# A hybrid attention block on one core: stores moved some steps behind their tiles, the loads of one value pass spread evenly, and eight chains shifted by five steps

## The chip, the cores and the metric

The kernel runs on one core of one Trainium2 chip. A core has a matrix engine (PE, with its weight loads listed as PEld), a vector engine (DVE), an activation engine (ACT), a general engine (POOL) and a sync engine (SP), and 16 DMA engines that move data between its working memory and the chip's main memory. SP, ACT and POOL each issue DMAs from their own queue of instructions. The metric is the time of one execution in microseconds (us), as the median of several runs; a profile of one more execution is beside it. Times inside an execution are counted from the start of its span.

## The reference

512 tokens of width 2048 go through one layer. `h = rmsnorm(x)` is projected by one wide matrix into the operands of two mixers and two gates; the mixers' outputs are projected, gated, merged, projected again and added to the residual.

```python
h = rmsnorm(x, norm_gain)
proj = h @ w_in
(aq, ak, av, az, iq, ik, iw, rq, rk, rv, rz, ga, gb) = jnp.split(proj, SPLIT_POINTS, axis=-1)
a_out = dsa_mixer(aq, ak, av, iq, ik, iw, positions, rel_bias) * jax.nn.silu(az)
b_out = retention_mixer(rq, rk, rv, ret_gn_gain) * jax.nn.silu(rz)
merged = jax.nn.sigmoid(ga) * (a_out @ w_a_out) + jax.nn.sigmoid(gb) * (b_out @ w_b_out)
r = x + merged @ w_o
return r + (p_i @ w_ple) * jax.nn.sigmoid(r @ w_ple_gate)      # then a last rmsnorm
```

Mixer A selects 128 keys for each query by an index score (`lax.top_k`) and attends to them with a bias that depends on the distance; mixer B is a retention with 8 heads in chunks of 64 tokens. All is float32. The kernel gets that precision from matmuls of a reduced form: each operand is split into a high part and a low part, and three products are added.

## The kernel before, in words

**Stages, in order of time.** (1) The index projection and its scores. (2) Four *values passes* (`values`, L685): two for the retention's values `rv`, two for the attention's values `av`. In a pass the split activations `hparts` (16 pairs of tiles, one pair per block k of the width) are the stationary operands, and a weight unit of 2 k is the moving one; k runs over 16 blocks, and for each k four token tiles t get three matmuls each. So a pass has 16 x 4 = 64 steps in 8 weight units, and ends with four accumulators that `normal` (L703, on ACT) scales out of PSUM. (3) 24 *pairs* (`gemm_pair`, L213): for each of 8 retention heads, one pair for its queries and keys, and two for gates. A pair computes two 128-column blocks of the projection with seven products of half size instead of eight; the products `s3, a11, a12, s4, s2, a22, s1` each have their own moving operands `Xh`, 8 tiles each, 56 in all. A product is one weight unit: 8 matmuls with the high weights and 8 with the low ones, 8 steps; a pair has 56 steps. (4) More pairs for `rz`, attention's `q`, `k` and `az`, then the attention heads and the output projections.

**The moving parts.** The 56 tiles of `Xh` are made from `x` in the background of the first passes (`combos`, L266) and stored to main memory (`hd`). `x_load(count)` (L824, issued by SP) brings them back, in the order of the products. Before, the third pass (i = 0) asks for `s // 4` tiles after block s, that is none in blocks 0 to 3 and three per block in 12 to 15, 24 in all; the fourth pass (i = 1) asks for two per block, 32. They take slots of one pool of 69 tiles (`U`, L51), which also holds `hparts`, the values' results and most scratch tiles. A slot is taken again only when the last user of its tile is done, a store among them; so the loads of the fourth pass also take slots that `hparts` leave.

**The order of work is written by hand.** The program's order on each engine is the order in which the Python code issues, and each engine takes its instructions in that order. `step()` (L164) is called after each group of matmuls; `later(n, f)` issues f n steps later. A background list `bg` (L154) holds the rest: the 48 steps that make the moving parts, 48 rounds of the top-k selection (L597 to L604, DVE), the mask's copy and store (`mask_store`, L609), and 160 steps that build the position bias (masks on DVE, L616; 12 small matmuls on PE, L630; a copy and a store on ACT, L633 to L637). One entry is issued every `state["rate"]` steps: 2 in the values passes, 20 in the 24 pairs, 9 after.

**Weights.** `load_to` (L106) has SP load blocks of 512 KB into 7 buffers, some units ahead of use; `split_to` (L121) has ACT write the high part `wh` (L136) two units ahead of its matmuls and one step later DVE the low part `wl` (L141); each has 3 buffers. In a pair, three of the seven units add another block of weights to the buffer: `add_block` (L102) does it with an accumulating DMA on POOL's queue.

**Around the change.** At the end of each `av` pass ACT scales the first accumulator to `avh`, stores it, then stores `avl`, which DVE makes from the same accumulator (L840), and so on for three token tiles; the fourth is stored whole (L837). The next pass, or the first pair, is issued after these. `retention(h)` (L713) hands its steps to `later` when the head's second output is there: `queries` (DVE), `scores` (PE, `ps_rs` L744), `keys`, `decay`, `states`, `values_out`, `norm` (with a POOL instruction, L796), `scale` and `back`, after which SP stores `yd` (L813). Before, `scores` comes 19 steps and `norm` 52 steps after it; the rotation of queries and keys ends on DVE with the instruction of L730, 7 steps after it. `b_load` (L1014) brings mixer B's result back for its output projection and 25 steps later has it split.

Of the kernel before, what the change touches and what calls it, by code (L numbers as in the profile page):

```python
# [9 lines left out]
F32 = mybir.dt.float32  # L10
F32R = mybir.dt.float32r
# [3 lines left out]
OP = mybir.AluOpType  # L15
# [5 lines left out]
NT = L // 128  # L21
# [13 lines left out]
def block_kernel(tc, xT, pT, posb, posq, w_in, w_v, w_ik, w_a, w_b, w_o, w_ple, w_gate,  # L35
                 w_gt, w_pt, fgb, tab, gains, cst, dec, out, out_a, out_b):
    nc = tc.nc
    pe, dve, act, pool, sp = nc.tensor, nc.vector, nc.scalar, nc.gpsimd, nc.sync

    with contextlib.ExitStack() as ctx:  # L40
# [10 lines left out]
        def U(name, dt=F32):  # L51
            return up.tile([128, L], dt, name=name, tag="u")
# [19 lines left out]
        state = {"raw": 0, "split": 0, "rate": BG_RATE}  # L72
# [85 lines left out]
        def later(n, f):  # L158
            if n <= 0:
                return f()  # L160
            tick[1] += 1
            heapq.heappush(soon, (tick[0] + n, tick[1], f))
# [153 lines left out]
        u_rv, u_av = ([block(w_v[i], (2,) * 8, 512) for i in g] for g in ((0, 1), (2, 3)))  # L316
# [24 lines left out]
        for k in range(KT):  # L341
            if k in (1, 2, 4, 8, 12):
                load_to(state["raw"] + 1)
            if k < 10:
                t = U("xk")
                sp.dma_start(t, xT[:, k, :])
                xs.append(t)
            elif k % 2 == 0:
                t = B("xk2")
# [92 lines left out]
        R = {}  # L442
# [164 lines left out]
        mnd = dp.tile([128, 1280], F32, name="mnd")  # L607

        def mask_store():  # L609
            t = B("mf")  # L610
            dve.tensor_copy(t, mneg)
            later(2, lambda: sp.dma_start(mnd, t))

        bias_e = {}

# [69 lines left out]
        def values(ids, name, each=lambda s: None):  # L685

            pss = [P("ps_vn") for _ in range(NT)]
            seq = ksteps(ids)
            for s, (i, k) in enumerate(seq):
                if k == 0:  # L690
                    split_to(i + AHEAD)
                    load_to(i + AHEAD + LOADS)
                h, l = loaded[i]
                a, b = hparts[s]
                for t in range(NT):
                    pe.matmul(pss[t], a[:, tok(t)], h[:, k], start=(s == 0), stop=False)  # L696
                    pe.matmul(pss[t], a[:, tok(t)], l[:, k], start=False, stop=False)  # L697
                    pe.matmul(pss[t], b[:, tok(t)], h[:, k], start=False, stop=(s == KT - 1))  # L698
                    step()
                each(s)  # L700
            return pss

        def normal(ps, name, t, dt=F32):  # L703
            v = U(name, dt)
            act.activation(v, ps, AF.Copy, scale=R["nat"][:, t:t + 1])
            return v
# [3 lines left out]
        vd = dp.tile([2, 7, 128, L], F32, name="vd")  # L710
        rd = dp.tile([2, NT, 128, L], F32, name="rd")

        def retention(h):  # L713
# [44 lines left out]
            def keys(i):  # L758
                if i == 0:
                    E["pk"] = turn(E[1], 3)  # L760
                else:
                    E["kn"] = U("kn")
                    act.activation(E["kn"][:, 0:384], E["pk"], AF.Copy, scale=dect[:, 256:257])

            def states(i):
                if i == 0:
                    ps = E["ps"] = P("ps_kv")
                    for t in range(3):
                        pe.matmul(ps[:, tok(t)], E["kn"][:, tok(t)], rv[:, tok(t)], start=True, stop=True)
                elif i == 1:  # L770
                    E["s"] = U("state")
                    act.activation(E["s"][:, 0:128], E["ps"][:, 0:128], AF.Copy)
                else:
                    for t in (1, 2):
                        dve.scalar_tensor_tensor(E["s"][:, tok(t)], E["s"][:, tok(t - 1)], g128, E["ps"][:, tok(t)],
                                                 op0=OP.mult, op1=OP.add)

            def values_out(t):
                if t == 0:
                    E["py"] = P("ps_y")  # L780
                    E["st"] = S("gst", 24)
                    E["mv"] = S("gmv", 8)
                o = E["py"][:, tok(t)]
                pe.matmul(o, E["at"][:, tok(t)], rv[:, tok(t)], start=True, stop=(t == 0))
                if t:
                    pe.matmul(o, E["qt"][:, tok(t - 1)], E["s"][:, tok(t - 1)], start=False, stop=True)
# [20 lines left out]
            def back(i):  # L807
                if i == 0:
                    E["pt"] = turn(E["yn"], NT)
                else:  # L810
                    E["yT"] = U("yT")
                    act.activation(E["yT"], E["pt"], AF.Copy, scale=gn[:, h:h + 1])
                    later(2, lambda: sp.dma_start(yd[h], E["yT"]))  # L813

            steps = [(9, queries), (19, scores), (21, lambda: keys(0)), (22, decay), (24, lambda: keys(1))]
            steps += [(n, lambda i=i: states(i)) for i, n in enumerate((34, 36, 38))]
            steps += [(46 + t, lambda t=t: values_out(t)) for t in range(NT)]
            steps += [(52, norm), (62, scale), (74, lambda: back(0)), (77, lambda: back(1))]
            return rotate

        Xh = {n: [None] * 8 for n in PRODUCTS}
# [2 lines left out]
        def x_load(count):  # L824
            while x_wanted and count:
                n, k = x_wanted.popleft()
                Xh[n][k] = U("h" + n, F32R)
                sp.dma_start(Xh[n][k].bitcast(F32), x_at[n, k])
                count -= 1
# [2 lines left out]
            for t, ps in enumerate(values(u_rv[i], "rv")):  # L832
                act.dma_start(rd[i, t], normal(ps, "rv", t))
        for i in range(2):
            for t, ps in enumerate(values(u_av[i], "av", lambda s, i=i: x_load(2 * i or s // 4))):
                if t == NT - 1:
                    act.dma_start(vd[i, 6], normal(ps, "av", t))  # L837
                    continue
                vh, vl = normal(ps, "avh", t, F32R), U("avl", F32R)
                dve.scalar_tensor_tensor(vl, ps, R["nat"][:, t:t + 1], vh.bitcast(F32), op0=OP.mult, op1=OP.subtract)  # L840
                act.dma_start(vd[i, 2 * t], vh.bitcast(F32))
                act.dma_start(vd[i, 2 * t + 1], vl.bitcast(F32))
        for i in range(len(x_wanted)):
            later(1 + 2 * i, lambda: x_load(1))
        state["rate"] = BG_RATES[1]


# [51 lines left out]
        av = []  # L899
# [114 lines left out]
        def b_load(h):  # L1014
            t = U("bk")
            sp.dma_start(t, bd[h])
            later(25, lambda: bparts.append(split(t, "b", 1)))

        for n in range(NH // 2):
            if n == NH // 2 - 1:  # L1020
                while bg:
                    bg.popleft()()
                for h in range(NH):
                    later(10 + 3 * h, lambda h=h: b_load(h))
                heads = [attention_head(h) for h in range(NH)]
                later(38, heads[0].pop(0)[1])
            gate_pair(u_az[n], to(zd[2 * n:2 * n + 2], AF.Silu))
# [27 lines left out]
        for m in PAIRED:  # L1055
            t = B("sm")
            s, o = t[:, 0:512], t[:, 512:1024]
# [17 lines left out]
        for m in range(8):  # L1075
# [13 lines left out]
            if m == 7:  # L1089
                todo.extend([None] * 24)  # L1090
                for k in range(2):
                    t = U("pk")
# [9 lines left out]
        for m in range(MF):  # L1102
            i = u_p[m // 4][0]
# [3 lines left out]
            h, l = loaded[i]  # L1107
            ps = P("ps_pw")
# [270 lines left out]
```

## Time and profile before

| what | value |
|---|---|
| median of 3 runs | 1722.48 us (1719.68 to 1722.67) |
| profiled execution, its own time | 1720.52 us |
| its span, first to last instruction | 1718.7 us |
| mean granted clock of PE | 0.994 |
| DVE, ACT, POOL busy | 1265.3, 867.3, 219.6 us |
| moved by DMA | 361.76 MB, 210 GB/s over the span |

The page gives each engine's busy time, the chain of work that ended last, and the costliest groups of instructions. A group's line gives the source line, engine, operation, output and inputs, the count, the busy time, and after the bar the idle time before it with what ended it. Other views are used too: the waits (who waited for whom, in all, how often, the longest), the timeline (start, length, instruction, and in square brackets the idle time before it and what ended it; "ACTq" and "SPq" are DMA issues from those queues), and windows (busy time of each engine, PE's granted clock as a share of full speed, and the mean busy share of the 16 DMA engines, in a stretch of time). Matmuls are pipelined: the start of one to the start of the next is what it takes, not its listed length.

### The profile page before, as it was taken

How to read it: one execution, taken by the hardware profiler on the slowest of the kernel's cores; microseconds unless marked ns; L12 is line 12 of the kernel's file. 1: busy time of each engine (PE TensorE's matmuls, PEld its weight loads, DVE VectorE, ACT ScalarE, POOL GpSimd, SP SyncE). 2: the span in 40 equal slices, each digit the busy share in tenths (PEclk: the TensorE clock that was granted, in tenths of full speed). 3: DMA queues.
4: the chain of work that ended last, by engine and by line, in shares of the span. 5: the costliest groups of instructions: out<-in, count | busy, mean ns of one | idle time of the engine just before them, and what ended most of it. 6: DMA issues, size and time to landing. Idle time of an engine off the chain costs nothing.

```text
span 1718.7 us, 25053 instructions
## 1 busy us (share of the span) xinstructions
PE 1690.7 (98%) x9334; PEld 1454.1 (85%) x9334; DVE 1265.3 (74%) x2007; ACT 867.3 (50%) x1288; POOL 219.6 (13%) x224
## 2 busy tenths in 40 slices
PE   9999989999999999999999999999999999999997
PEld 7988877788888888888888888888888888888896
DVE  7787985777878778877787776776668877864453
ACT  7465422455555555555555545566644444463342
POOL 2100000111111111111331111100000111112222
PEclk9999999999999999999999999999999999999999
DMA  7338979787787787787898888899856688732222
GB/s 283 123 116 293 355 269 293 201 219 198 190 220 201 193 215 201 194 214 206 229 236 232 224 214 222 229 309 366 273 201 205 172 214 223 205 121 100 91 68 98
DMA packets 136665, 361.76 MB, mean 210 GB/s; under 512 B 14944, under 2 KB 27232, under 8 KB 136544
## 3 DMA queue, kind: packets, MB, share of 16 engines
q1 hardware_dynamic: 98176, 251.63, 42.1%
q0 software_dynamic: 22528, 82.85, 26.8%
q10 hardware_dynamic: 15840, 25.70, 4.2%
q8 instruction: 73, 1.20, 0.3%
q14 instruction: 48, 0.39, 0.1%
HBM read 306.51 MB, written 53.61 MB: 210 GB/s over the span
## 4 chain that ended last, share of the span: by engine, by line
PE 81%; DVE 8%; DMA 7%; ACT 2%; issue 1%; SPq 0%; ACTq 0%; POOL 0%; DVEq 0%; POOLq 0%
PE ps_p L258 22%; PE ps_v L258 14%; PE ps_r L258 8%; PE ps_q L258 7%; PE ps_pg L198 3%; PE ps_pg L197 3%; PE ps_pg L196 3%; PE ps_w L197 2%; PE ps_w L196 2%; PE ps_w L198 2%; DVE isc L601 1%; DVE wl L141 1%; PE ps_iq L196 1%; PE ps_iq L197 1%; PE ps_iq L198 1%
## 5 line engine op out<-in xcount | busy, mean ns | idle before, releaser
L141 DVE TENSOR_TENSOR wl<-wraw,wh 128x1024 fp32r<-128x1024 f32 (+2 forms) x459 | 560.3, 1229 | 234.2 <-ACT wh L136 227.6
L136 ACT ACTIVATE wh<-wraw 128x1024 fp32r<-128x1024 f32 (+2 forms) x459 | 474.3, 1042 | 250.7 <-DVE wraw L143 116.1
L104 POOL DMA_DIRECT2D wraw<-w_in x120 | 105.8, 943 | 914.3 <-DVE wl L141 352.1
L224 ACT ACTIVATE e<-ps_p 128x512 f32<-128x512 f32 x144 | 86.1, 598 | 176.8 <-PE ps_p L258 174.4
L258 PE MATMUL ps_p<-hs,wh 128*128 128x512 f32 x640 | 161.5, 393 | 0.0
L258 PEld LDWEIGHTS ps_p<-hs,wh 128*128 128x128 f32 x640 | 114.7, 189 | 21.6 <-issue 1.3
L696 PE MATMUL ps_vn<-wh,hh 128*128 128x512 f32 x256 | 101.3, 396 | 4.7 <-ACT wh L136 4.7
L697 PE MATMUL ps_vn<-wl,hh 128*128 128x512 f32 x256 | 100.9, 394 | 0.5 <-DVE wl L141 0.5
L698 PE MATMUL ps_vn<-wh,hl 128*128 128x512 f32 x256 | 100.6, 393 | 0.0
L258 PE MATMUL ps_p<-hs,wl 128*128 128x256 f32 x640 | 96.6, 287 | 0.0
L258 PE MATMUL ps_q<-ha,wh 128*128 128x512 f32 x320 | 84.5, 401 | 3.4 <-ACT wh L136 3.4
L258 PEld LDWEIGHTS ps_p<-hs,wl 128*128 128x128 f32 x640 | 83.9, 192 | 1.1 <-issue 1.1
L258 PE MATMUL ps_p<-ha,wh 128*128 128x512 f32 x320 | 80.8, 393 | 0.0
L258 PE MATMUL ps_r<-hs,wh 128*128 128x512 f32 x320 | 80.5, 393 | 0.0
L258 PE MATMUL ps_v<-ha,wh 128*128 128x512 f32 x320 | 80.3, 391 | 0.0
L258 PE MATMUL ps_v<-hs,wh 128*128 128x512 f32 x320 | 79.6, 390 | 0.0
L198 PE MATMUL ps_pg<-rh,wl 128*128 128x512 f32 x192 | 74.8, 390 | 0.0
L197 PE MATMUL ps_pg<-rl,wh 128*128 128x512 f32 x192 | 74.7, 389 | 0.0
L196 PE MATMUL ps_pg<-rh,wh 128*128 128x512 f32 x192 | 74.7, 389 | 0.0
L857 DVE TENSOR_TENSOR go<-e_t 128x256 f32<-128x256 f32 x160 | 68.0, 425 | 5.6
L258 PEld LDWEIGHTS ps_v<-ha,wh 128*128 128x128 f32 x320 | 59.8, 188 | 13.6 <-issue 1.2
L258 PEld LDWEIGHTS ps_v<-hs,wh 128*128 128x128 f32 x320 | 59.9, 188 | 13.1 <-ACT wh L136 0.4
(352 smaller groups left out, 3521.5 us busy)
## 6 DMA issues: line engine op xcount, KB each, us to landing
wraw<-w_in SPq DMA_DIRECT2D x174, 512.0 KB, 4.9
wraw<-w_in POOLq DMA_DIRECT2D x120, 512.0 KB, 7.6
wraw<-w_v SPq DMA_DIRECT2D x32, 512.0 KB, 4.5
wraw<-w_o SPq DMA_DIRECT2D x32, 512.0 KB, 4.9
wraw<-w_o POOLq DMA_DIRECT2D x24, 512.0 KB, 6.8
wraw<-w_gate SPq DMA_DIRECT2D x24, 512.0 KB, 3.8
hd<-hs SPq DMA_DIRECT2D x32, 256.0 KB, 4.7
hs<-hd SPq DMA_DIRECT2D x32, 256.0 KB, 5.5
```

The source lines that it names most:

```text
L104: pool.dma_start(out=raw_tiles[r], in_=src[:, k0:k0 + 8, :], accum_op=OP.add)
L136: act.activation(h, raw, AF.Copy)
L141: dve.tensor_sub(l, raw, h.bitcast(F32))
L196: pe.matmul(o, h[:, k, w], a, start=(s == order[0]), stop=False)
L197: pe.matmul(o, h[:, k, w], b, start=False, stop=False)
L198: pe.matmul(o, l[:, k, w], a, start=False, stop=(s == order[-1]))
L224: act.activation(E[n], src, AF.Copy)
L258: pe.matmul(o[:, c], w[:, k], X[PRODUCTS[n]][k][:, c], start=(n < 4 and part == 0 and k == 0), stop=(part == parts[1] and k == 7), skip_gr ...
L696: pe.matmul(pss[t], a[:, tok(t)], h[:, k], start=(s == 0), stop=False)
L697: pe.matmul(pss[t], a[:, tok(t)], l[:, k], start=False, stop=False)
L698: pe.matmul(pss[t], b[:, tok(t)], h[:, k], start=False, stop=(s == KT - 1))
L857: dve.tensor_add(o[:, q], c0, c1)
```

## The change

It edits six places.

- `mask_store`: the DMA that stores the mask is issued 20 steps after the copy that makes its tile, not 2.
- `retention`: `scores` and all later steps of a head come 5 steps later (19 to 24, and so on to 77 to 82); `queries` stays at 9.
- The third pass asks for one moving part per block k (16 in all, before 24), the fourth for two as before (32); the 8 that remain, all of the last product `s1`, are asked for in the first pair, one every 3 steps.
- In the fourth pass the background goes at one entry per 4 steps (`BG_RATE`), not 2.
- After an `av` pass, the four `normal` instructions are issued on ACT one behind the other, then the three `avl` on DVE, and the seven stores are issued on ACT 8, 10, ... 20 steps later.
- `b_load`: head h at 4 + 3h steps, before 10 + 3h.

```diff
         def mask_store():
             t = B("mf")
             dve.tensor_copy(t, mneg)
-            later(2, lambda: sp.dma_start(mnd, t))
+            later(20, lambda: sp.dma_start(mnd, t))
...
-            steps = [(9, queries), (19, scores), (21, lambda: keys(0)), (22, decay), (24, lambda: keys(1))]
-            steps += [(n, lambda i=i: states(i)) for i, n in enumerate((34, 36, 38))]
-            steps += [(46 + t, lambda t=t: values_out(t)) for t in range(NT)]
-            steps += [(52, norm), (62, scale), (74, lambda: back(0)), (77, lambda: back(1))]
+            steps = [(9, queries), (24, scores), (26, lambda: keys(0)), (27, decay), (29, lambda: keys(1))]
+            steps += [(n, lambda i=i: states(i)) for i, n in enumerate((39, 41, 43))]
+            steps += [(51 + t, lambda t=t: values_out(t)) for t in range(NT)]
+            steps += [(57, norm), (67, scale), (79, lambda: back(0)), (82, lambda: back(1))]
...
         for i in range(2):
-            for t, ps in enumerate(values(u_av[i], "av", lambda s, i=i: x_load(2 * i or s // 4))):
-                if t == NT - 1:
-                    act.dma_start(vd[i, 6], normal(ps, "av", t))
-                    continue
-                vh, vl = normal(ps, "avh", t, F32R), U("avl", F32R)
-                dve.scalar_tensor_tensor(vl, ps, R["nat"][:, t:t + 1], vh.bitcast(F32), op0=OP.mult, op1=OP.subtract)
-                act.dma_start(vd[i, 2 * t], vh.bitcast(F32))
-                act.dma_start(vd[i, 2 * t + 1], vl.bitcast(F32))
+            if i:
+                state["rate"] = BG_RATE
+            pss = values(u_av[i], "av", lambda s, i=i: x_load(i + 1))
+            vs = [normal(ps, "av", t, F32 if t == NT - 1 else F32R) for t, ps in enumerate(pss)]
+            for t in range(NT - 1):
+                vl = U("avl", F32R)
+                dve.scalar_tensor_tensor(vl, pss[t], R["nat"][:, t:t + 1], vs[2 * t].bitcast(F32), op0=OP.mult,
+                                         op1=OP.subtract)
+                vs.insert(2 * t + 1, vl)
+            for j, v in enumerate(vs):
+                later(8 + 2 * j, lambda v=v, j=j, i=i: act.dma_start(vd[i, j], v if j == 6 else v.bitcast(F32)))
         for i in range(len(x_wanted)):
-            later(1 + 2 * i, lambda: x_load(1))
+            later(1 + 3 * i, lambda: x_load(1))
...
                 for h in range(NH):
-                    later(10 + 3 * h, lambda h=h: b_load(h))
+                    later(4 + 3 * h, lambda h=h: b_load(h))
```

## The prediction

> **What bounds the kernel now.** I read the page first, for the engine that is full, and the chain of work that ended last.
>
> ```profile
> PE 1690.7 (98%) x9334; PEld 1454.1 (85%) x9334; DVE 1265.3 (74%) x2007; ACT 867.3 (50%) x1288; POOL 219.6 (13%) x224
> PE 81%; DVE 8%; DMA 7%; ACT 2%; issue 1%; SPq 0%; ACTq 0%; POOL 0%; DVEq 0%; POOLq 0%
> q1 hardware_dynamic: 98176, 251.63, 42.1%
> q0 software_dynamic: 22528, 82.85, 26.8%
> ```
>
> PE is full, and the change takes no matmul away. So it can only give back time in which PE stands or runs slowly, and the second view is PE's own waits.
>
> ```profile
> PE ps_vn L696 <- ACT wh L136: 4.7, 1, 4.7
> PE ps_rs L744 <- DVE go L730: 4.1, 3, 3.5
> PE ps_q L258 <- ACT wh L136: 3.4, 1, 3.4
> PE ps_w L197 <- DVE bl L676: 1.5, 1, 1.5
> PE ps_bias L630 <- DVE mk L622: 0.6, 1, 0.6
> ```
>
> Five short rows, 14.3 us together, and each is at a place that the diff touches. But a wait costs more than its length, which PE's timeline shows around the first of them, in the fourth values pass:
>
> ```profile
> 247.44 0.39 PE L698 MATMUL ps_vn<-wh,hl 128*128 128x512 f32 x1
> 252.55 0.80 PE L696 MATMUL ps_vn<-wh,hh 128*128 128x512 f32 x1 [4.72 <-ACT wh L136]
> ...
> 254.40 0.63 PE L698 MATMUL ps_vn<-wh,hl 128*128 128x512 f32 x1
> 254.83 0.63 PE L696 MATMUL ps_vn<-wh,hh 128*128 128x512 f32 x1
> ...
> 258.65 0.40 PE L696 MATMUL ps_vn<-wh,hh 128*128 128x512 f32 x1
> ```
>
> After the stop the starts are 0.43 us apart until 258.65, where a clean pass has 0.227 (43.5 us for its 192 matmuls). From 247.44 to 258.65 there are 13 intervals, which should take 2.9 us and take 11.2: the wait of 4.7 costs 8.3. The next view gives whole pairs: the first rows below are the starts of the first, second, and third pair of head 0, then the second and third pair of head 1, then the last pair before the output projection and that projection.
>
> ```profile
> 290.96 0.63 PE L258 MATMUL ps_v<-hs,wh 128*128 128x512 f32 x2
> 315.66 0.98 PE L258 MATMUL ps_v<-hs,wh 128*128 128x512 f32 x3
> 326.82 2.04 PE L744 MATMUL ps_rs<-go 128*128 128x128 f32 x8 [3.45 <-DVE go L730]
> 344.53 0.62 PE L258 MATMUL ps_v<-hs,wh 128*128 128x512 f32 x2
> ...
> 384.50 0.62 PE L258 MATMUL ps_v<-hs,wh 128*128 128x512 f32 x2
> 408.27 0.62 PE L258 MATMUL ps_v<-hs,wh 128*128 128x512 f32 x2
> ...
> 1117.75 0.62 PE L258 MATMUL ps_v<-hs,wh 128*128 128x512 f32 x2
> 1137.27 0.39 PE L196 MATMUL ps_w<-bh,wh 128*128 128x512 f32 x1
> ```
>
> A clean pair takes 1137.27 - 1117.75 = 19.5 us; the first takes 24.7, so 5.2 too much. Head 1's second pair, which carries a head's retention steps, takes 23.8; head 0's takes 28.9, 5.1 too much. In pairs a step is 19.5 / 56 = 0.35 us, in values passes 43.5 / 64 = 0.68 us.
>
> **The change part by part.** *Stores behind their tiles, third pass.* Why ACT was late with `wh` stands in ACT's and DVE's timelines:
>
> ```profile
> 235.67 0.33 ACTq L841 DMA_DIRECT2D vd<-avh  x1
> 246.22 0.33 ACTq L842 DMA_DIRECT2D vd<-avl  x1
> 246.60 0.69 ACT L705 ACTIVATE avh<-ps_vn,r_nat 128x512 fp32r<-128x512 f32 x1 [10.96 <-DVE avl L840]
> ...
> 251.44 2.95 ACT L136 ACTIVATE wh<-wraw 128x1024 fp32r<-128x1024 f32 x3 [0.40 <-ACT av L705]
> ```
>
> ```profile
> 239.43 1.22 DVE L141 TENSOR_TENSOR wl<-wraw,wh 128x1024 fp32r<-128x1024 f32 x1
> 245.44 0.75 DVE L840 SCALAR_TENSOR_TENSOR avl<-ps_vn,r_nat,avh 128x512 fp32r<-128x512 f32 x1
> ```
>
> DVE runs about 10 us behind (the selection rounds at one entry per 2 steps fill it), the store of `avl` stands on ACT until DVE is there, and three `wh` stand behind it. After the change four `normal` at 0.69 us end near 238, and `wh` of the pass's unit 2 follows at once; PE wants it at 247.7. The same seven stores are still issued, but 5.4 to 13.6 us later, when their tiles exist; behind each stands `wh` of a unit that PE wants 10 us later. What is late next is DVE: three `avl` at 0.75 from 245.44, then `wl` of unit 2 at 1.22, done at 248.9, and PE wants it 0.23 after 247.7. That leaves a wait of 1.0 us, with 0 (if DVE is a little less behind) and 3.5 (if a little more) as ends. With one entry per 4 steps DVE then has 1.2 + 2 x 1.1 us of work per unit of 5.4 and catches up. **Gain 8.3 - 1.0 = 7.3.** The slower rate moves three bias groups out of this pass; they and their matmuls are issued later, so that is worth only the wait of 0.6 on `mk`: **0.6**.
>
> *First and second pair.* The windows show what the DMA engines did:
>
> ```profile
> 237.00:247.00 10.00, 10.00 (x46) 8.27 (x45) 8.95 (x21) 0.40 (x1) 0.00 (x0) 1.00 0.40 137
> ...
> 291.00:316.00 25.00, 21.59 (x114) 18.33 (x113) 11.25 (x14) 10.19 (x14) 0.89 (x1) 0.93 1.00 326
> ```
>
> The last two columns are the share of the DMA engines and GB/s. They are at 0.40 in the stretch in which ACT's store is held, and at 1.00 from 291 to 316, when what was not asked for earlier comes at once. What holds SP's queue besides is in its waits:
>
> ```profile
> SPq L813 <- ACT yT L812: 127.6, 8, 16.9
> SPq L612 <- DVE mk L622: 11.5, 1, 11.5
> ```
>
> ```profile
> 272.60 0.32 SPq L612 DMA_DIRECT2D mnd<-mf  x1
> ```
>
> The mask's store keeps SP waiting for 11.5 us up to 272.6, and the loads behind it bunch up. In the first pair the weights then land late, and ACT and DVE are late for the rotation:
>
> ```profile
> 306.15 0.89 POOL L104 DMA_DIRECT2D wraw<-w_in  x1 [17.46 <-DMA wraw<-w_in]
> ```
>
> ```profile
> 314.55 2.01 ACT L136 ACTIVATE wh<-wraw 128x1024 fp32r<-128x1024 f32 x2 [3.82 <-DMA wraw<-w_in]
> ```
>
> With the store 20 steps behind its copy, the loads spread, and the stores off the end of the pass, the causes of the 5.2 and the 5.1 go. In their place come, all in the first pair, the eight `s1` tiles (steps 1 to 22), the seven `vd` stores (steps 8 to 20) and the mask's store: of the 32 background entries of the fourth pass before, 12 were selection rounds and the next was the mask's copy; at one per 4 steps the copy comes at step 52 of 64, and its store at step 8 of the pair. Their price follows from the queues. On q1 a MB takes 0.421 x 1718.7 / 251.63 = 2.88 us of all 16 engines, on q0, which carries POOL's adding loads, 0.268 x 1718.7 / 82.85 = 5.6.
>
> ```profile
> wraw<-w_in POOLq DMA_DIRECT2D x120, 512.0 KB, 7.6
> hs<-hd SPq DMA_DIRECT2D x32, 256.0 KB, 5.5
> vd<-avh ACTq DMA_DIRECT2D x6, 256.0 KB, 4.8
> ```
>
> Up to the last `s1` tile: 8 tiles and 7 stores of 0.26 MB, the mask 0.66, the head's constants and values 0.4, three weight blocks 1.6 make 6.6 MB or 19 us, one adding load 2.9: 22 us. PE reaches that tile 6 x 2.79 + 0.9 = 17.6 us into the pair. So it comes 4 us late if all of it goes before, and in time if the last stores and weights pass behind. ACT, which issues the stores, may also be held by them and be late with `wh` of the sixth unit (wanted at 14.0), for 0 to 3 us. I take **a new wait of 3.5 us** in all; ends 0 and 9 (9 with a backlog from the fourth pass, where 32 tiles, 7 stores and five weight blocks make 12.8 MB, with three adding loads 46 us of DMA in a pass of 44.5). **Gain 5.2 + 5.1 - 3.5 = 6.8.**
>
> [...]
>
> *Scores five steps later.* 1.75 us of slack more per head, where DVE was late once more: the row of `ps_rs` has 4.1 in 3 waits, 3.5 of it in head 0. **Gain 0.5** in the other heads. What is moved with it: POOL's `norm` passes behind one adding load whose block landed long before, and the store of `yd` on SP, which is weighed as a rival. *b_load* six steps (2.1 us) earlier: the split that PE waits 1.5 for is then ahead of the pair's last DVE work: **1.5**, ends 0 and 1.5.
>
> **Sum:** 7.3 + 0.6 + 6.8 + 0.5 + 1.5 = 16.7 us. The profiled execution took 1720.5, so 1703.8; it lies 2.0 below the median of the runs, 1722.5, and against that the forecast is **1705.8**.
>
> **Rivals.** *Transfers bind the first pair.* The stretch at a share of 1.00 only moves: the new wait is 9, with half clock 10.5, and the gain 16.7 - 7.0 = 9.7: **1712.8**. For it: 22 us of transfers before a tile wanted at 17.6. Against it: the fourth pass leaves gaps to fill (0.40 at 237 to 247). [...] *DVE takes ACT's place in the fourth pass:* `wl` is 3.5 late and the clock halves, 5.5 in all instead of 1.0: **1710.3**. *It does not do what it says:* ACT's stores are still held, now by transfers in flight, and as much is lost as before: **1722**. *Slower:* the store of `yd` holds SP 5 steps longer in every head, and weights stand behind it:
>
> ```profile
> 353.25 0.39 SPq L115 DMA_DIRECT2D wraw<-w_in  x1
> ```
>
> ```profile
> 371.48 1.05 ACT L136 ACTIVATE wh<-wraw 128x1024 fp32r<-128x1024 f32 x1
> ```
>
> This block is issued right after the store and landed some 5 us later; by the order of units its `wh` is at 371.48, 13 us later, so 1.75 us do not reach it. If the slack in some heads were below 1.75, each head would pay what the second pair paid: 8 x 5.1 = 41, so **1747**.
>
> **Chances.** Forecast 0.62, transfers bind 0.18, DVE 0.09, no effect 0.03, slower 0.08. Range 1700 to 1714: below, no new wait in the pair and none in the fourth pass (1701.3), above, the rivals of transfers and DVE (1712.8), and about 1 us on each side for the spread of the runs. A difference of 0.2% (3.4 us) is about what can be told from no change here. Faster by more 0.89, within 0.03, slower 0.08.
>
> **What would show it.** In the changed profile: no row of `ps_vn` waiting for `wh`; a short one for `wl` near 248; the first pair starting near 281; `ps_rs` without waits; in the first pair, PE waits of `ps_p` for a moving tile or for `wh`. It is wrong if the first pair is longer than 29 us, or if pairs of later heads pass 24.5.

## The result, and the profile after

The kernel after takes 1706.87 us in the median (1706.01 to 1707.68), the kernel before 1722.48 (1719.68 to 1722.67). The ratio is 0.9913, with a 95% interval of 0.9896 to 0.993: 0.9% faster, 1.1 us above the forecast. The profiled execution after took 1707.68, the highest of its runs, and the one before 1720.52, 2.0 below its median; so between the two profiles there are only 12.8 us (spans 1718.7 and 1705.9), between the medians 15.6.

The page of the kernel after, the lines that were shown of before:

```profile
PE 1685.2 (99%) x9334; PEld 1451.1 (85%) x9334; DVE 1264.7 (74%) x2007; ACT 865.4 (51%) x1288; POOL 220.1 (13%) x224
...
q1 hardware_dynamic: 98176, 251.63, 43.2%
q0 software_dynamic: 22528, 82.85, 26.7%
...
PE 83%; DMA 7%; DVE 7%; ACT 2%; issue 1%; SPq 0%; ACTq 0%; POOL 0%; DVEq 0%
```

The work is the same: as many matmuls and as many bytes. Only the time in which PE stands or is slow has changed. Its waits, in the kernel after (in all, how often, the longest):

```profile
PE ps_p L258 <- DVE wl L141: 2.7, 1, 2.7
PE ps_vn L697 <- DVE wl L141: 1.7, 1, 1.7
...
PE ps_v L258 <- ACT wh L136: 1.5, 1, 1.5
...
PE ps_p L258 <- DMA hs<-hd: 0.6, 1, 0.6
```

The rows of `ps_vn` waiting for `wh` (4.7), `ps_rs` for the rotation (4.1), `ps_q` for `wh` (3.4) and `ps_w` for `bl` (1.5) are gone; three have come, and the one of `ps_vn` for `wl`, 0.5 before, has grown to 1.7. Where they stand is seen in PE's timeline after, at the start of the fourth pass, its wait, the starts of the first three pairs, the start of `rz`, and that of the output projection:

```profile
236.43 0.39 PE L696 MATMUL ps_vn<-wh,hh 128*128 128x512 f32 x1
...
249.42 0.50 PE L697 MATMUL ps_vn<-wl,hh 128*128 128x512 f32 x1 [1.72 <-DVE wl L141]
249.76 0.40 PE L698 MATMUL ps_vn<-wh,hl 128*128 128x512 f32 x1
250.00 0.40 PE L696 MATMUL ps_vn<-wh,hh 128*128 128x512 f32 x1
...
282.00 0.84 PE L258 MATMUL ps_v<-hs,wh 128*128 128x512 f32 x3
...
295.97 1.21 PE L258 MATMUL ps_p<-hs,wl 128*128 128x256 f32 x8 [2.66 <-DVE wl L141]
...
300.51 2.12 PE L258 MATMUL ps_v<-ha,wh 128*128 128x512 f32 x8 [1.49 <-ACT wh L136]
...
304.88 0.89 PE L258 MATMUL ps_p<-hs,wl 128*128 128x256 f32 x2 [0.58 <-DMA hs<-hd]
...
307.44 0.39 PE L258 MATMUL ps_v<-hs,wh 128*128 128x512 f32 x1
...
330.93 0.63 PE L258 MATMUL ps_v<-hs,wh 128*128 128x512 f32 x2
...
795.02 0.61 PE L258 MATMUL ps_v<-hs,wh 128*128 128x512 f32 x2
...
1124.18 0.39 PE L196 MATMUL ps_w<-bh,wh 128*128 128x512 f32 x1
```

From such starts, us:

| stage | before | after | change |
|---|---|---|---|
| start of the fourth pass | 236.79 | 236.43 | -0.4 |
| fourth values pass | 54.17 | 45.57 | -8.6 |
| first pair | 24.70 | 25.44 | +0.7 |
| second pair | 28.87 | 23.48 | -5.4 |
| rest of the 24 pairs | 466.28 | 464.10 | -2.2 |
| pairs from `rz` to the last | 326.46 | 329.16 | +2.7 |
| B's output projection, attention heads | 128.19 | 128.28 | +0.1 |
| from A's output projection to the last matmul | 446.64 | 447.00 | +0.4 |

In the fourth pass ACT (timeline after) now has the four `normal` in one piece, with `wh` of the pass's units 1 and 2 behind them (237.22 and 242.07):

```profile
234.59 2.73 ACT L705 ACTIVATE av<-ps_vn,r_nat 128x512 fp32r<-128x512 f32 x4 [2.34 <-PE ps_vn L698]
236.78 0.33 ACTq L845 DMA_DIRECT2D vd<-av  x1
237.22 1.05 ACT L136 ACTIVATE wh<-wraw 128x1024 fp32r<-128x1024 f32 x1
242.07 1.06 ACT L136 ACTIVATE wh<-wraw 128x1024 fp32r<-128x1024 f32 x1 [3.80 <-PE ps_vn L698]
246.94 0.33 ACTq L845 DMA_DIRECT2D vd<-avl  x1
```

DVE is still some 10 us behind, as the timeline of DVE after shows, and ACT's store of `avl` still stands until DVE has been there (246.94), but no `wh` that PE wants soon stands behind it:

```profile
246.16 2.07 DVE L841 SCALAR_TENSOR_TENSOR avl<-ps_vn,r_nat,av 128x512 fp32r<-128x512 f32 x3
248.15 1.22 DVE L141 TENSOR_TENSOR wl<-wraw,wh 128x1024 fp32r<-128x1024 f32 x1
```

The first pair is where the time did not come. ACT after, in it:

```profile
290.59 0.33 ACTq L845 DMA_DIRECT2D vd<-avl  x1
...
292.74 0.33 ACTq L845 DMA_DIRECT2D vd<-av  x1
293.12 0.60 ACT L224 ACTIVATE e<-ps_p 128x512 f32<-128x512 f32 x1 [6.59 <-DMA mnd<-mf]
293.61 1.05 ACT L136 ACTIVATE wh<-wraw 128x1024 fp32r<-128x1024 f32 x1
```

ACT stood for 6.6 us. By the profile its store at 290.59 went out as the one issued at 282.35 landed, 8.16 us later, and its next activation, at 293.12, ended a wait for the mask's store, which SP had issued at 283.23 and which took 9.4 us to land; the `wh` behind came only at 293.61. The other way round, SP's waits from 270 to 310 have one of 4.4 us at `vd<-av`, a store of ACT. So the profile puts waits of each queue down to a transfer that the other had issued; by what means one holds the other is not shown.

### The profile page after: what moved, and what is told of

Read it like the earlier page. It is cut to its first block, busy times and chain, and to the rows that moved or that the text cites. A ratio compares the mean times of both kernels' runs of the same rounds, so it can differ in the third digit from the quotient of the medians.

```text
span 1705.9 us, 25048 instructions
## 1 busy us (share of the span) xinstructions
PE 1685.2 (99%) x9334; PEld 1451.1 (85%) x9334; DVE 1264.7 (74%) x2007; ACT 865.4 (51%) x1288; POOL 220.1 (13%) x224
## 4 chain that ended last, share of the span: by engine, by line
PE 83%; DMA 7%; DVE 7%; ACT 2%; issue 1%; SPq 0%; ACTq 0%; POOL 0%; DVEq 0%
PE ps_p L258 23%; PE ps_v L258 15%; PE ps_r L258 8%; PE ps_q L258 7%; PE ps_pg L198 3%; PE ps_pg L197 3%; PE ps_pg L196 3%; PE ps_w L197 2%; PE ps_w L196 2%; PE ps_w L198 2%; DVE wl L141 1%; PE ps_iq L196 1%; PE ps_iq L197 1%; PE ps_iq L198 1%; PE ps_vn L697 1%; DVE isc L601 1%
## 5 line engine op out<-in xcount | busy, mean ns | idle before, releaser
L258 PE MATMUL ps_p<-hs,wh 128*128 128x512 f32 x640 | 167.4, 397 | 0.0
L258 PE MATMUL ps_p<-hs,wl 128*128 128x256 f32 x640 | 91.5, 284 | 3.4 <-DVE wl L141 2.7
L258 PE MATMUL ps_r<-hs,wh 128*128 128x512 f32 x320 | 85.8, 400 | 0.0
L258 PEld LDWEIGHTS ps_v<-hs,wh 128*128 128x128 f32 x320 | 60.0, 188 | 12.8 <-issue 0.2
```

The lines of the kernel that those rows point to most:

```text
L258: pe.matmul(o[:, c], w[:, k], X[PRODUCTS[n]][k][:, c], start=(n < 4 and part == 0 and k == 0), stop=(part == parts[1] and k == 7), skip_gr ...
```

## The experiments

Two theories stood against each other at each place. For the fourth pass: the *stores* on ACT ahead of `wh`, or the slower background *rate*. For the pairs: *volume* (too much is to be moved in the first pair), or ACT *held* by its own stores; and, for what had been wrong before, late weights, or too few steps of slack. With each run stands in brackets the kernel that its edit is made to; the code is cut to the lines that matter, with `...` where lines are left out. The stages of all runs, us, from the matmuls' starts in each profile, and the medians (a ratio is to the kernel before as it ran beside that kernel, with medians of 1721.6 to 1722.5):

| kernel | 4th pass | 1st pair | 2nd pair | rest of 24 | rz to last | median | ratio to before, interval |
|---|---|---|---|---|---|---|---|
| before | 54.17 | 24.70 | 28.87 | 466.28 | 326.46 | 1722.48 | |
| b_stores | 48.97 | 22.13 | 30.06 | 466.20 | 326.49 | 1713.84 | 0.9962 (0.9948 to 0.9977) |
| b_five | 54.41 | 26.47 | 25.53 | 464.74 | 326.49 | 1716.33 | 0.9968 (0.9955 to 0.9981) |
| b_mask | 53.46 | 23.79 | 28.78 | 466.17 | 326.49 | 1718.50 | 0.9985 (0.9975 to 0.9994) |
| after | 45.57 | 25.44 | 23.48 | 464.10 | 329.16 | 1706.87 | 0.9913 (0.9896 to 0.993) |
| a_now | 50.55 | 27.92 | 23.53 | 464.10 | 329.17 | 1715.84 | 0.9969 (0.9959 to 0.998) |
| a_rate2 | 48.18 | 26.70 | 24.48 | 464.74 | 326.49 | 1709.36 | 0.9932 (0.9917 to 0.9947) |
| a_no_five | 44.29 | 25.40 | 23.45 | 465.43 | 329.15 | 1707.05 | 0.9919 (0.9902 to 0.9936) |
| a_bload10 | 43.89 | 25.63 | 23.51 | 464.10 | 329.17 | 1706.95 | 0.9915 (0.9899 to 0.993) |
| a_sp | 44.45 | 26.81 | 23.55 | 464.10 | 329.17 | 1706.88 | 0.9912 (0.9896 to 0.9927) |
| a_loads | 44.39 | 19.51 | 25.31 | 464.10 | 329.15 | 1701.59 | 0.9886 (0.9866 to 0.9905) |
| a_even24 | 45.35 | 19.51 | 25.36 | 464.10 | 329.15 | 1702.16 | 0.9885 (0.9869 to 0.9901) |
| c_mask | 44.69 | 19.51 | 25.08 | 464.10 | 329.15 | 1702.17 | 0.9887 (0.9871 to 0.9903) |
| c_rates | 43.52 | 19.51 | 25.22 | 463.99 | 328.67 | 1699.49 | 0.9871 (0.9855 to 0.9887) |

The fourth pass is the same in a_no_five, a_bload10, a_sp and after, in code and order; it took 43.9 to 45.6 us. So its last 1.7 us vary from one execution to the next, and a single profile doesn't size a term finer there.

**b_stores**, the deferred stores alone (to the kernel before):

```
-            for t, ps in enumerate(values(u_av[i], "av", lambda s, i=i: x_load(2 * i or s // 4))):
...
+            pss = values(u_av[i], "av", lambda s, i=i: x_load(2 * i or s // 4))
+            vs = [normal(ps, "av", t, F32 if t == NT - 1 else F32R) for t, ps in enumerate(pss)]
...
+            for j, v in enumerate(vs):
+                later(8 + 2 * j, lambda v=v, j=j, i=i: act.dma_start(vd[i, j], v if j == 6 else v.bitcast(F32)))
```

> The kernel before with one part of the change: the seven stores behind their tiles after both av passes, the four scalings first. Loads, background rate, mask store, retention steps, b_load as before. Theory (the store of avl stood on ACT ahead of wh): the fourth values pass falls from 54.2 us to 46 to 47.5 (at the rate of one entry per 2 steps DVE is further behind, so the wait for wl is 1.9 or more), the first and second pair stay at 25 to 27 and 28 to 29; about 1715. Rival (the slower background rate relieves DVE, and the stores only looked guilty): the fourth pass stays at 53 to 55, and the time at 1722.

**a_now**, the stores at once again, each behind its tile's scaling, all else of the change kept (to the kernel after):

```
-            for j, v in enumerate(vs):
-                later(8 + 2 * j, lambda v=v, j=j, i=i: act.dma_start(vd[i, j], v if j == 6 else v.bitcast(F32)))
...
+                act.dma_start(vd[i, 2 * t], vh.bitcast(F32))
+                act.dma_start(vd[i, 2 * t + 1], vl.bitcast(F32))
```

> The kernel after with the stores issued at once again, each behind its tile's scaling, as before; everything else of the change stays, the slower background rate of the fourth pass among it. Theory (stores on ACT ahead of wh): the fourth pass goes back to 53 to 55 us from 45.6, and the time to about 1715. Rival (the background rate): it stays at 46 to 48, and the time within 2 us of 1706.9.

Both speak for the stores. Alone they take 5.2 us off the fourth pass; taken back alone they give 5.0 back. The waits of PE in a_now, and its ACT timeline, have the old picture at the slow rate too:

```profile
PE ps_vn L696 <- ACT wh L136: 4.1, 1, 4.1
```

```profile
245.44 0.33 ACTq L844 DMA_DIRECT2D vd<-avl  x1
245.81 0.69 ACT L705 ACTIVATE avh<-ps_vn,r_nat 128x512 fp32r<-128x512 f32 x1 [10.32 <-DVE avl L842]
```

The rival isn't empty, though: b_stores has 49.0 where 46 to 47.5 was expected, and a_now 50.6 where 53 to 55 was; the rest goes with the rate. That the stores also take 2.6 us off the first pair (22.13 for 24.70) and add 1.2 to the second (30.06 for 28.87) was in neither expectation.

**a_rate2**, the fourth pass at one background entry per 2 steps (to the kernel after):

```
-            if i:
-                state["rate"] = BG_RATE
```

> The kernel after with the background rate of the fourth pass back at one entry per 2 steps. Theory (the rate matters little for the pass's start, since DVE's backlog there comes from the third pass): the fourth pass 45.5 to 47; the three bias groups come back into it, with a wait of 0.6 for their mask, and the pairs at the end, where they were pushed to, lose the 2.8 us that one of them gained; the mask's copy is ahead of the first pair, so its store of 0.66 MB leaves it, and the first pair falls from 25.4 to about 24. About 1705 to 1707. Rival (the rate relieved DVE): the fourth pass at 50 or more, and about 1711.

Neither fits. The median is 2.5 us worse, and the runs of the two kernels don't overlap (1707.9 to 1710.8, 1706.0 to 1707.7); the fourth pass is 2.6 longer, the two pairs 2.3, and the later pairs give 2.0 back, where three groups of bias work now are not. That the pairs suffer was in neither theory. SP's waits in a_rate2, from 258 to 305, suggest why:

```profile
SPq L828 <- DMA scr<-bev: 11.2, 3, 7.1
```

By the profile SP's loads of moving parts wait there, 11.2 us in all, until stores of the position bias (`scr<-bev`, issued by ACT) have landed. In the kernel after, at the slower rate, the first such store comes at 325.0, well behind the first pair, as the view of that line shows (first and last start):

```profile
L637 ACTq DMA_DIRECT2D scr<-bev x32: 525/526/597, 325.0 to 1095.1; - x32
```

In a_rate2 the last load for the product `a22` is issued at 284.62, as the first pair starts (284.51); in the kernel after it is issued at 276.12, 5.9 us ahead of it. This is read from the trace, not shown by a run that moves these stores alone. All of SP's waits from 258 to 305 add up to the same 32 us in both kernels: what differs is what SP waits for, and which loads stand behind.

**b_mask**, the mask's store 20 steps behind its copy, alone (to the kernel before):

```
-            later(2, lambda: sp.dma_start(mnd, t))
+            later(20, lambda: sp.dma_start(mnd, t))
```

> The kernel before with one part of the change: the mask's store 20 steps behind its copy. Theory M (the store holds SP for 11.5 us, the weights behind it are late in the first pair and the rotation in the second): SP's wait for the mask's copy goes, the first pair falls from 24.7 us to 20 to 22, the second from 28.9 to 24 to 26; about 1713 to 1716. Rival (late weights have another cause; the store only meets the loads somewhat later): first and second pair together stay at 52 to 54 us, about 1721.

Theory M falls: first and second pair together 52.6 us, before 53.6. The median is 3.2 us lower (1718.50 for 1721.65), between the two forecasts, and the profile puts only 1.0 of that into the pairs and 0.7 into the fourth pass. The wait of 11.5 at the mask's store is gone, but SP's waits from 262 to 300 in b_mask have others in its place:

```profile
SPq L828 <- DMA scr<-bev: 10.9, 2, 8.5
SPq L828 <- DMA hs<-hd: 5.1, 6, 2.8
SPq L718 <- DMA scr<-bev: 3.1, 1, 3.1
```

One hold of SP stood in front of another. So the edit pays little alone; that it pays together with the rate, which moves the bias stores out, is likely but no run has the two as a pair.

**b_five**, the five steps alone (to the kernel before), and **a_no_five**, all but the five steps (to the kernel after):

```
-            steps = [(9, queries), (19, scores), (21, lambda: keys(0)), (22, decay), (24, lambda: keys(1))]
...
+            steps = [(9, queries), (24, scores), (26, lambda: keys(0)), (27, decay), (29, lambda: keys(1))]
```

> The kernel before with one part of the change: the retention's steps from scores on five steps later. Undone alone in the kernel after, this part was worth nothing in the second pair (23.45 us without it, 23.48 with it). Theory (the second pair loses its 5.1 us because the rotation comes late from the first pair; either cure, earlier weights or five steps of slack, removes most of it): the second pair falls from 28.9 us to 24.5 to 26, the wait of ps_rs from 3.5 to about 1.7 with no half clock behind it; other heads 1.3 less; about 1717 to 1718. Rival (the five steps do nothing there, the weights are late in any case): second pair 28 or more, and 1721.

> The kernel after with the retention's steps where they were (scores at 19). Theory (the second pair was late because of bunched loads; five steps of slack are worth 0.5 us in all): second pair 23.5 to 24.5 us, a wait of ps_rs of up to 1 us, about 1707 to 1708. Rival (the five steps did it): the second pair is back at 28 to 29 us, about 1712.

Alone the five steps take 3.3 us off the second pair and 1.5 off the pairs behind it; the first pair, which the edit does not reach, is 1.8 longer in that profile, with a wait for `wh` of 4.0 in place of 3.4 and a granted clock of 0.63 from 298 to 300. In b_five's waits `ps_rs` no longer stands; a shorter one is left in the second pair:

```profile
PE ps_q L258 <- DVE wl L141: 1.2, 1, 1.2
```

Taken away from the kernel after, they cost nothing in the second pair (23.45) and 1.3 in the others, and the median moves by 0.2. So the second pair has two cures, the five steps (most of it) and something else in the change (all of it), and the kernel after has both.

**a_loads** and **a_even24**, the moving parts requested as before, or 24 of them evenly, in both cases none left for the first pair (to the kernel after):

```
-            pss = values(u_av[i], "av", lambda s, i=i: x_load(i + 1))
+            pss = values(u_av[i], "av", lambda s, i=i: x_load(2 * i or s // 4))
```

```
-            pss = values(u_av[i], "av", lambda s, i=i: x_load(i + 1))
+            pss = values(u_av[i], "av", lambda s, i=i: x_load(2 if i else 1 + s % 2))
```

> The kernel after with the moving parts requested as before: s // 4 per k in the third pass (24), two per k in the fourth (32), none in the first pair. Theory V (volume: the tiles left for the first pair are what makes it 25.4 us): first pair 21 to 22.5 us, as in the kernel before with the stores alone deferred (22.1), and the second pair stays at 23.5 to 25; about 1704. Rival B (bunched loads late in the third pass and in the fourth make the weights late, which is what the change cured): second pair 27 or more, fourth pass 46 or more, about 1710.

> The kernel after with 24 moving parts in the third pass (one and two per k in turn), 32 in the fourth, none in the first pair. Theory V (volume in the first pair): 2 MB leave it, 6 us of all DMA engines, so the gaps of 0.9 and 0.5 for moving tiles go and the two waits behind ACT's held stores shrink: first pair 21 to 23 us from 25.4, about 1703 to 1704. Rival A (ACT is held by its own stores whatever SP loads): 24.5 or more, and 1706. If the third pass has no free tiles for 8 more, SP stands, weights come late, and the third pass grows by more than 1 us.

**a_sp**, the seven stores behind the fourth pass on SP's queue (to the kernel after):

```
-                later(8 + 2 * j, lambda v=v, j=j, i=i: act.dma_start(vd[i, j], v if j == 6 else v.bitcast(F32)))
+                later(8 + 2 * j, lambda v=v, j=j, i=i: (sp if i else act).dma_start(vd[i, j], v if j == 6 else v.bitcast(F32)))
```

> The kernel after with the seven stores that follow the fourth pass issued on SP's queue and not on ACT's, at the same steps. Theory A (ACT is held by its own stores, which wait for transfers in flight, and is then late with wh): the waits for wl (2.7) and for wh (1.5) in the first pair go, 21.5 to 22.5 us from 25.4, about 1703.5. Rival V (volume: whoever issues the stores, the weights and tiles behind them come late): SP stands instead, and with it loads of tiles and weights: 25 or more, 1707 or more.

Volume decides. With the eight tiles gone the first pair takes 19.51, a clean pair, better than the 21 to 22.5 that its own theory expected (the second is 1.8 longer, 25.3); with the stores on another queue it takes 26.8 and the median stays. Bunched or even makes no difference (1701.6 and 1702.2): what counts is that 24 tiles are fetched in the third pass, not 16. The windows show where the room was: the last quarter of the third pass, and the first pair. In the kernel after (last two columns: share of the DMA engines and GB/s):

```profile
225.00:237.00 12.00, 12.00 (x55) 9.93 (x54) 11.69 (x30) 4.53 (x6) 0.00 (x0) 1.00 0.58 180
282.00:307.00 25.00, 20.14 (x112) 16.93 (x111) 13.48 (x17) 10.58 (x14) 2.02 (x3) 1.00 1.04 340
```

The same in a_loads:

```profile
225.00:237.00 12.00, 12.00 (x54) 9.93 (x54) 11.69 (x29) 5.04 (x7) 0.00 (x0) 1.00 0.95 332
282.00:307.00 25.00, 25.00 (x145) 22.04 (x144) 16.17 (x22) 10.76 (x15) 3.52 (x4) 1.00 1.02 323
```

At 225 to 237 the DMA engines were at 0.58 with the one-per-k request and at 0.95 with the old one, at no cost to PE (12.00 busy in both). From 282 to 307 they are full in both kernels, but PE is busy 25.00 of 25 us in the one and 20.14 in the other. The one-per-k request takes 2 MB (8 x 0.26) out of a stretch with room and puts them into a full one: it costs 4.7 to 5.3 us of the median. How they make weights late stands in SP's timeline from 279 to 300, first in the kernel after, then in a_loads:

```profile
285.77 0.33 SPq L115 DMA_DIRECT2D wraw<-w_in  x1
289.50 4.17 SPq L828 DMA_DIRECT2D hs<-hd  x3
294.76 0.33 SPq L115 DMA_DIRECT2D wraw<-w_in  x1
```

```profile
284.10 12.64 SPq L115 DMA_DIRECT2D wraw<-w_in  x6
```

In both kernels most of SP's waits from 258 to 305 end, by the profile, with the landing of an earlier transfer: 30.8 of 32.3 us in the kernel after, 24.8 of 31.0 in a_loads. In the kernel after, tiles stand between the blocks of weights (the blocks at 285.77 and 294.76 are 9 us apart); in a_loads six blocks go out within 12.6 us. Whether the tiles' bytes or their places in SP's queue count for more, the runs don't split.

**a_bload10**, `b_load` six steps later, as before (to the kernel after):

```
-                    later(4 + 3 * h, lambda h=h: b_load(h))
+                    later(10 + 3 * h, lambda h=h: b_load(h))
```

> The kernel after with b_load six steps later, as before. The stage from the first matmul of mixer B's output projection to the first of mixer A's took 128.19 us before and 128.28 after, and 127.3 to 128.8 in the other kernels of this study. Theory (the wait for the split of 1.5 comes back and nothing goes): 129.5 to 130 us, about 1708. Rival (other waits in that stage take the place of the one removed, so the edit is worth nothing): 127.5 to 128.8, within 1 us of 1706.9.

The wait of `ps_w` for `bl` is back with its 1.5, the stage (B's output projection and the attention heads) takes 129.17, not 128.28, and the median stays (1706.95). It lies between the two expectations. In the nine kernels with the early `b_load` the stage takes 127.3 to 128.8, so one profile can't size the difference, and the medians show none.

**c_mask** and **c_rates**, towards a better version (c_mask to a_loads, c_rates to c_mask):

```
-            later(20, lambda: sp.dma_start(mnd, t))
+            later(110, lambda: sp.dma_start(mnd, t))
```

```
-            pss = values(u_av[i], "av", lambda s, i=i: x_load(2 * i or s // 4))
+            pss = values(u_av[i], "av", lambda s, i=i: (state.update(rate=BG_RATE if i or s > 11 else 2), x_load(2 * i or s // 4)))
...
-BG_RATES = (2, 20, 9)
+BG_RATES = (2, 20, 8)
```

> The kernel after with two edits: moving parts requested as before (24 bunched in the third pass, 32 in the fourth, none in the first pair) and the mask's store 110 steps behind its copy, which puts it some 50 steps into the second pair or later and takes 0.66 MB, 1.9 us of all DMA engines, out of the first. The first alone gave 1701.6 with a clean first pair and 25.3 us for the second, in which weights come late. Theory (volume ahead of the second pair's weights): the second pair 23.0 to 24 us, 1700 to 1701. Rival (they are late because the first pair is now as short as it can be and the seven stores alone fill the DMA engines): 25 us or more, 1701.6.

> The kernel of the run c_mask (moving parts as before, mask's store 110 steps behind) with two edits of the background rate: one entry per 4 steps already in the last quarter of the third pass, so DVE is some 4 us less behind when the fourth starts, and 8 steps per entry, not 9, in the stages after the 24 pairs, so that no bias groups are left to be issued at once at the end. Theory: the wait for wl in the fourth pass (0.6 to 1.7 in the runs) goes, the pass takes 43.5 to 43.8 us; the last pairs lose the wait for the mask of 0.5; 1698.5 to 1700. Rival (what is left out of the third pass only comes back as DVE and PE work in the pairs): within 0.7 us of c_mask.

In c_mask it comes out as the rival said: the second pair stays at 25.1, so the mask's 0.66 MB ahead of it is not what makes its weights late. That the seven stores do, the rival's reason, is not shown. In c_rates the theory holds: the fourth pass is clean (43.52) and the pairs from `rz` to the last lose 0.5; 1699.49 us (1698.0 to 1700.47), 7.4 below the kernel after, and the fastest of all. DVE's timeline in c_rates has `wl` of unit 2 3.6 us earlier than the kernel after, ahead of PE's need:

```profile
244.56 1.22 DVE L141 TENSOR_TENSOR wl<-wraw,wh 128x1024 fp32r<-128x1024 f32 x1
```

## Why the prediction was right, and where it was not

The time was right (1705.8 forecast, 1706.87 measured) and so were the signs named for the profile; several terms were not, and their errors cancel in part. That the medians come within 1.1 us is partly luck: from profile to profile, on which the sum was built, the gain is 12.8 us, not 16.7, because the profiled execution before was 2.0 below its median and the one after 0.8 above.

*Fourth pass*, 7.3 and 0.6 forecast, 8.6 measured. The mechanism is shown by b_stores and a_now. The term was 8.3 - 1.0; the wait for `wl` came where it was named, as 1.72 at 249.42, which with PE's delay behind it is 1.9. Over the kernels with the same order it is 0.4 to 2.0, so the 1.0 was a fair middle. (`wh` of unit 2 did not follow at once, near 238, but at 242.07; that was early enough.) Before, the pass was 10.7 over a clean one: 8.3 for the stop and 2.4 else, bias work with its wait above all; with the slower rate that work comes back as 2.7 in the pairs from `rz` on. The rival that DVE takes ACT's place with a halved clock did not happen: the granted clock was 1.00 from 247 to 259.

*The rate* was priced at 0.6 for one wait. It is worth 2.5 (a_rate2). The step that failed is "they and their matmuls are issued later, so that is worth only the wait": it counted the bias groups as work for DVE and PE, and left out that each ends in a store. The two pairs are 2.3 us longer with these stores ahead of them, and SP's loads wait 11.2 us for them; that the one causes the other is argued from the trace. The work itself is only moved, as was said: from the third pair to the output projection a_rate2 is 2.0 us shorter than the kernel after.

*First and second pair*, "5.2 + 5.1 - 3.5". Measured 4.6 less instead of 6.8: the new waits made the first pair 5.9 longer than a clean one, not 3.5, within the ends of 0 and 9, so that it rose to 25.4 where 23.0 was forecast. The cause of the new wait, volume, was right, down to the late last `s1` tiles; but the first stop was for `wl` of the fifth unit (2.66), where the prediction had named `wh` of the sixth (1.49), and that it brought no half clock was luck, as a_bload10 shows below. What the rival of transfers adds for half clock, 10.5 less 9, is a term that no run shows; measured were a clock of 0.50 for 3.41 us behind a wait of 2.77 in a_bload10, and of 1.00 behind the 2.66 in the kernel after. Of the old waits the prediction counted three cures together, the mask's store later, "the loads spread", and the stores off the end of the pass. The step that failed is the second: in a_loads the loads are asked for in bunches, as before, and the first pair is clean, so spreading them cured nothing and made the new wait. The mask's store alone is worth 1.0 of the 10.3 (b_mask), the stores alone 1.4 (b_stores: 2.6 off the first pair, 1.2 more in the second). What made the pairs late before looks like a queue of holds: ACT's stores at the end of the pass, the mask's copy, the bias stores behind it. The runs don't split it further: rate and mask were not tried as a pair alone.

*The second pair* got its 5.4, but five steps alone give 3.3 of it, where the prediction counted none. That the other cure in the kernel after is the first pair's own delay, in which weights and DVE get ahead, is argued, not shown: wherever the first pair is clean, the second is 25.1 to 25.4; where it takes 25.4 or more and the parts are spread, 23.5 to 24.5.

*Scores five steps later* in other heads: 0.5 forecast, 1.3 to 1.5 in the stage. *b_load*: 1.5 forecast; the wait went and the stage did not get shorter (128.19 and 128.28), so the term was nothing that can be measured. *The slower rival*, SP held longer by the store of `yd`, was half right, as SP's waits in the kernel after show:

```profile
SPq L115 <- DVE yn L803: 100.5, 7, 15.5
...
SPq L813 <- ACT yT L812: 40.5, 8, 5.2
```

Before, the store alone had 127.6 in 8 waits, and there was no row for `yn`; in a_no_five, without the five steps, it has 126.4 again and no such row. Now a weight load stands ahead of the store and takes most of the wait; together they are 141.0, 1.7 us more per head, which is the five steps. What did not follow is its price: the weights were still early enough, and the later heads' second pairs went from 23.14 to 24.27 us to 23.03 to 23.70.

## What to carry to other kernels

When loads are spread out, ask which stretch they leave and which they enter: here 2 MB left a stretch in which the DMA engines then stood at 0.58, for one in which they were full (1.04), and it cost about 5 us, however even it looked. A store that waits for a slow engine belongs behind the work that others want soon, and when one hold of a queue is removed, list what else holds the same queue, other engines' stores among them, before its length is booked as gain. And undo each part alone: here one part of a change that gained 0.9% was a loss.

## What the runs showed of the hardware

Two waits of nearly the same length left PE's clock differently. In the kernel after, the wait of 2.66 at 295.97 left the granted clock at 1.00. In a_bload10 the same wait, 2.77 long, was followed by 0.50, as PE's timeline and then its windows show (PE's busy time is the second figure, the granted clock the third from the right):

```profile
293.99 1.75 PE L258 MATMUL ps_p<-hs,wl 128*128 128x256 f32 x8 [2.77 <-DVE wl L141]
```

```profile
290.99:294.41 3.42, 0.65 (x5) 0.45 (x5) 1.67 (x2) 1.54 (x2) 0.00 (x0) 1.00 1.05 268
294.41:297.82 3.41, 3.41 (x13) 2.93 (x12) 2.09 (x4) 0.33 (x1) 0.00 (x0) 0.50 1.04 393
297.82:301.23 3.41, 3.40 (x18) 2.59 (x17) 2.64 (x4) 3.41 (x5) 0.00 (x0) 1.00 1.04 378
```

The same in the kernel after, around its wait:

```profile
291.55:294.96 3.41, 1.76 (x12) 1.44 (x10) 0.27 (x1) 1.54 (x2) 0.00 (x0) 1.00 1.06 332
294.96:298.38 3.42, 2.41 (x14) 2.18 (x15) 2.38 (x3) 0.00 (x0) 0.00 (x0) 1.00 1.04 332
```

In a_bload10 the whole wait falls into a stretch of 3.41 us with 0.65 us of PE's work, and the next 3.41 us run at 0.50. In the kernel before the granted clock was 0.50 from 251.79 to 258.62, from 299.58 to 302.99 and from 326.89 to 330.30; in the 3.41 us ahead of these falls PE had 0.00, 0.54 and 0.07 us of work, as the profile lists it. So half clock also followed stretches in which PE was not idle throughout.

In the kernel after, the two stretches shown meet inside the wait, and neither has less than 1.76 us of work. That they are to be laid so is an estimate of the author, from the times of the clock's changes: the six times above are 2, 12, 1, 7 and 1 times 3.41 us apart; in the kernel after the clock fell only at 1697.84, and 294.96 lies 411 such steps ahead of that. Laid the same way, the new wait of the fourth pass stands in a stretch with 1.69 us of work, 247.18 to 250.59, and the clock stayed at 1.00 behind it. What decides it is not shown by these runs.
